# A third PSUM bank for projection tiles beside a recurrence, another order at the end of the attention, and more filling at one level

## The chip, the cores and the metric

The kernel runs on one NeuronCore of a Trainium2 chip. The metric is the device time of one execution in microseconds. TensorE (PE) multiplies matrices into PSUM, which is used here in banks of 128 x 512 float32; VectorE (DVE), ScalarE (ACT) and GpSimd (POOL) work on SBUF and PSUM, each through its own instructions in order; SyncE (SP) issues the DMA transfers.

## The reference, cut to what matters

One decoder layer over 16 meta tokens and 1024 tokens, D = 1024, all in float32. Four differential-attention heads and four heads of a gated linear recurrence (HGRN2) read one input projection; their outputs go side by side through an output projection, and a convolutional feed-forward part follows.

```python
a = rmsnorm(h, ln_mix_pre[l])
proj = a @ w_in[l]
dq, dk, dv, hq, hf, hi, hg = jnp.split(proj, SPLITS, axis=-1)
y_diff = diff_attention(dq, dk, dv, diff_lambda[l], diff_subln[l], rel_bias_table, lam_init)
y_hgrn = hgrn2(hq, hf, hi, hg, lb_all[l], hgrn_gnorm[l])
mix = jnp.concatenate([y_diff, y_hgrn], axis=-1) @ w_out[l]
h = h + rmsnorm(mix, ln_mix_post[l])
a = rmsnorm(h, ln_ffn_pre[l])
y = conv_ffn(a, w_ffn_up[l], ffn_conv_w[l], ffn_conv_b[l], w_ffn_down[l])
h = h + rmsnorm(y, ln_ffn_post[l])

# in diff_attention, for a block of 128 queries and a head, two maps m:
s = jnp.einsum('bhmqd,bhmkd->bhmqk', qblk, kh).astype(f32) * scale + bias[None, :, None]
s = jnp.where(dist >= 0, s, -jnp.inf)
p = jax.nn.softmax(s, axis=-1)
attn = p[:, :, 0] - lam * p[:, :, 1]
return jnp.einsum('bhqk,bhkd->bhqd', attn, vh)

# in hgrn2, for each position, with decay f = lb + (1 - lb) * sigmoid(f_logit):
S_new = jnp.exp(G_last)[..., None] * S + jnp.einsum(
    'bhsk,bhsv->bhkv', kh * jnp.exp(G_last[:, :, None] - G), vh)
```

## The kernel before, in words

A float32 product is made of three fp32r matmuls (high x high, low x high, high x low), so every weight tile is loaded, cast to its high half on ACT (`wh_...`), and its low half is a subtraction (`wl_...`, on POOL for the input projection, `wol...` on DVE for the output projection, where the high half is `woh...`).

The tokens lie in nine blocks: block 0 is the 16 meta tokens, the others 128 each. For the projections they make three groups of three blocks (`GROUPS`), of 272, 384 and 384 columns. A projection tile of a head (`dq`, `dk`, `dv` of the attention, `hf`, `hq`, `hi`, `hg` of the recurrence) is 24 matmuls per group into one PSUM bank, `pi_<name>_<group>` (`proj_group`, L231, and `proj_step`, L239). When the last of them is issued, the reading instructions follow: for dq, dk and dv ACT's casts to `q` and `k` and DVE's differences `q` and `kl`, or ACT's copy `vt`.

PSUM has eight banks: two are handed out in turn for the projection tiles (`ps_in`), two for small products (`ps_m`: `pl`, `pk`, `pu`, `pt`, `pa`, `E`), and four make two pairs for the scores and the recurrence's outputs (`ps_s`: `S`, `po`).

The order on TensorE is the order of the code. `interleave(dense, sides, fill, lead)` (L63) puts projection matmuls between the steps of a side: when a side yields a number c, matmuls for `fill` x c ns of nominal cost are issued, a matmul of 384 columns counting 161 and one of 272 counting 115; `FA, FH, FO` are 840, 800 and 800. The order on the other engines is chosen by the scheduler from the dependences, and each of them then runs its instructions one after another.

The main loop (L913 on) goes over the heads. The attention of head h is interleaved with the projection of the recurrence of head h; the recurrence of head h is interleaved with the projection of the attention of head h + 1, for heads 0 to 2. The recurrence of the last head is interleaved with the first part of the output projection (`py`, L988 to L992), whose token blocks are split in `mm<block>_<k>` (ACT's high half, DVE's low half) and read back through a DRAM buffer as `mp`.

In the recurrence (`hgrn_head`, L411) a tree of decay products is applied in seven levels. A level (`level`, L440 on) has 50 or fewer small matmuls `pl_<level>` of `kr` and `mix`, then multiplies `kr` by the decay (one instruction) and `mix` by it (one instruction for each of three groups, here called mix0, mix1 and mix2), and copies the results of the matmuls to `a` and `am`. The products of a level use the updates of the level before; each level ends with `yield 3`, so about 2400 ns of projection matmuls follow it. Behind level 7 three chains run side by side: transposes of `kr` (`pk`, L518), the state products (`pu`), the outputs (`po`) and their norms.

In the attention (`attn`) the last block of queries (block 8) has 1040 columns; its scores are in a pair of banks (`S`, 528 columns) and a small-product bank (`E`, 512 columns). Its maximum is the minimum of two negated maxima, one for `S` and one for `E` (`ast`, DVE, 128x1), and the two exponentials on ACT write the map `pb`. In the same stretch the transposes of block 7 (`pt_7`) are copied to `at_7` on DVE or ACT, and block 7's product `pa_7` follows. Behind that the two maps are combined on DVE (`pb`, 1040 columns) and block 8 is transposed.

Elsewhere in DVE's order stand the sums of the feed-forward weights (`wd`, one 128x512 addition at a time), and in POOL's order the splits `wl_...` of later tiles.

Of the kernel before, what the change touches and what calls it, by code (L numbers as in the profile page):

```python
# [13 lines left out]
ALU = mybir.AluOpType  # L14
# [12 lines left out]
NBLK = 9  # L27
# [7 lines left out]
FA, FH, FO = 840, 800, 800  # L35


def start(i):
    return 0 if i == 0 else META + P * (i - 1)


def rows(i):
    return META if i == 0 else P
# [17 lines left out]
def interleave(dense, sides, fill, lead=0):  # L61
    sides = list(sides)
    live = True  # L63

    def feed(budget):
        nonlocal live
        while live and budget > 0:
            c = next(dense, False)
            if c is False:
                live = False  # L70
            elif c is None:
                return
            else:
                budget -= c

    feed(lead)
    while sides:
        for s in list(sides):
            c = next(s, False)
            if c is False:  # L80
                sides.remove(s)
                continue
            feed(fill * (c or 1))
    feed(1e12)
# [3 lines left out]
def layer_kernel(ctx: ExitStack, tc: tile.TileContext, x, meta, table, lbl, gpre, gpost, win,  # L88
# [3 lines left out]
    V, A = Ordered(tc, nc.vector, state), Ordered(tc, nc.scalar, state)  # L92
# [53 lines left out]
    def ps_in(name):  # L146
        return pp.tile([P, 512], F32, tag="ip", name=name)
# [4 lines left out]
    def ps_s(name):  # L152
        return pp.tile([P, 2, 512], F32, tag="S", name=name)
# [70 lines left out]
    wd_sums = down_sums()  # L224
# [3 lines left out]
    def load_m(m, name, where=None, bufs=4):  # L228
        return [load_split(win[m][:, 512 * c: 512 * (c + 1)], f"{name}_{c}", where, bufs) for c in range(2)]

    def proj_group(g, parts, name, evac):  # L231
        b0, b1 = GROUPS[g]
        t0, t1 = start(b0), start(b1 - 1) + P
        n = t1 - t0
        pt = ps_in(f"pi_{name}_{g}")
        for k in range(KD):
            yield from proj_step(pt[:, :n], parts, k, t0, t1, lambda: evac(g, b0, b1, t0, t1, pt[:, :n]))

# [133 lines left out]
    def carried():  # L372
        tails = list(carry)
        carry.clear()
        return tails
# [37 lines left out]
    def hgrn_head(t, done=None):  # L413
        h, f, kr, vn = t["h"], t["f"], t["kr"], t["vn"]
# [88 lines left out]
        yield 3  # L503
        for lev in range(1, 8):
            level(lev)
            yield 3

        states = {0: None}

# [114 lines left out]
    def attn(h, tens):  # L624
        qs, ks, vn, rr = tens
        SY.dma_start(rr, rsc[h][127:127 + P * 383].rearrange("(p c) -> p c", c=383)[:, :256])
        pend = {}

        def scores(i):
            r = rows(i)  # L630
            q0 = start(i)
            W = q0 + r
            nm = f"{h}_{i}"
            pb = ap_.tile([P, 2, L], F32, tag="pb", name=f"pb{nm}", bufs=2)
            st = ap_.tile([P, 12], F32, tag="st", name=f"ast{nm}", bufs=3)
            pend[i] = pb
            nearw = min(256, W)
            j0 = P if i == 0 else 256 - nearw

            def qk_mm(dst, m, c0, n):  # L640
                T.matmul(dst, qs[m][:, q0:q0 + P], ks[m][:, c0:c0 + n], start=True, stop=False)
                T.matmul(dst, qs[m][:, q0:q0 + P], kl[m][:, c0:c0 + n], start=False, stop=True)

            nmx, sm, rc = st[:r, 0:2], st[:r, 2:4], st[:r, 4:5]
            if W <= 512:
                S = ps_s(f"S{nm}")
                for m in range(2):
                    qk_mm(S[:, m, :W], m, 0, W)
                near = S[:r, :, W - nearw:W]
                V.tensor_tensor(near, near, rr[:r, j0:j0 + nearw].rearrange("p (o c) -> p o c", o=1).to_broadcast([r, 2, nearw]), op=ALU.add)  # L650
                V.tensor_reduce(nmx, S[:r, :, :W], axis=AX.X, op=ALU.max, negate=True)
                for m in range(2):
                    A.activation(pb[:r, m, :W], S[:r, m, :W], AF.Exp, bias=nmx[:, m:m + 1], accum_out=sm[:, m:m + 1])
            else:
                for m in range(2):
                    S = ps_s(f"S{nm}_{m}")
                    hw = (W if W <= 912 else 528) // 2
                    for p_ in range(2):
                        qk_mm(S[:, p_, :hw], m, p_ * hw, hw)
                    mx = nmx[:, m:m + 1]  # L660
                    if W <= 912:
                        near = S[:r, 1, hw - 256:hw]
                        V.tensor_tensor(near, near, rr[:r], op=ALU.add)
                        V.tensor_reduce(mx, S[:r, :, :hw], axis=AX.XY, op=ALU.max, negate=True)
                        A.activation(pb[:r, m, :W].rearrange("p (a c) -> p a c", a=2), S[:r, :, :hw], AF.Exp, bias=mx, accum_out=sm[:, m:m + 1])
                    else:
                        E = ps_m(f"E{nm}_{m}")
                        qk_mm(E, m, 528, 512)
                        V.tensor_tensor(E[:r, 256:], E[:r, 256:], rr[:r], op=ALU.add)
                        ex = st[:r, 6 + 2 * m:8 + 2 * m]  # L670
                        V.tensor_reduce(ex[:, 0:1], S[:r, :, :hw], axis=AX.XY, op=ALU.max, negate=True)
                        V.tensor_reduce(ex[:, 1:2], E[:r], axis=AX.X, op=ALU.max, negate=True)
                        V.tensor_tensor(mx, ex[:, 0:1], ex[:, 1:2], op=ALU.min)
                        A.activation(pb[:r, m, :528].rearrange("p (a c) -> p a c", a=2), S[:r, :, :hw], AF.Exp, bias=mx, accum_out=ex[:, 0:1])
                        A.activation(pb[:r, m, 528:W], E[:r], AF.Exp, bias=mx, accum_out=ex[:, 1:2])
                        V.tensor_tensor(sm[:, m:m + 1], ex[:, 0:1], ex[:, 1:2], op=ALU.add)
                    if m == 0:
                        yield 0.7
            V.reciprocal(rc, sm[:, 1:2])
            V.scalar_tensor_tensor(rc, sm[:, 0:1], nlam[:r], rc, ALU.mult, ALU.mult)  # L680
            V.scalar_tensor_tensor(pb[:r, 0, :W], pb[:r, 1, :W], rc, pb[:r, 0, :W], ALU.mult, ALU.add)
            pend["sum", i] = sm[:, 0:1]
            yield 1.3 if W <= 512 else 0.7

        def values(i):
            r = rows(i)
            q0 = start(i)
            W = q0 + r
            nm = f"{h}_{i}"
            pb = pend.pop(i)  # L690
            pieces = [list(range(j, min(j + 4, i + 1))) for j in range(0, i + 1, 4)]
            ats = []
            for pi, blks in enumerate(pieces):
                pt = ps_m(f"pt{nm}_{pi}")
                at = ap_.tile([P, len(blks) if pi == 2 else 4, P], F32, tag=f"at{pi // 2}", name=f"at{nm}_{pi}", bufs=2 - pi // 2)
                for jj, j in enumerate(blks):
                    b = rows(j) if i == 0 else P
                    T.transpose(pt[:b, jj * r:(jj + 1) * r], pb[:r, 0, start(j):start(j) + b], ident[:r, :r])
                pv = pt.rearrange("p (j q) -> p j q", j=4)[:, :, :r] if r == P else None
                n0 = len(blks)  # L700
                if pi == 0:
                    A.copy(az[i % 2][:META, :r], pt[:META, :r])
                lo = 1 if pi == 0 else 0
                if n0 > lo:
                    (A.copy if pi % 2 else V.tensor_copy)(at[:, lo:n0], pv[:, lo:n0])
                ats.append(at)
                yield 0.8 if i < 4 else 0.6
            pend["ats"] = ats, pieces
# [44 lines left out]
                yield from values(i + 1)  # L753
        carry.append(pend.pop("tail"))

    def dense(tiles, preload=None, side=iter(())):
        parts = preload
        for idx, (m, name, evac) in enumerate(tiles):
            if parts is None:
                parts = load_m(m, name)  # L760
            nxt = load_m(tiles[idx + 1][0], tiles[idx + 1][1]) if idx + 1 < len(tiles) else None
            for g in range(3):
                next(side, None)
                for step, c in enumerate(proj_group(g, parts, name, evac)):
                    if step == 8:
                        flush()
                    yield c
            parts = nxt

    t_a, tiles = attn_in(0)  # L770
    parts = []
# [25 lines left out]
    pt = ps_m("pg")  # L797
# [12 lines left out]
    parts = [[None, None], [None, None]]  # L810
# [103 lines left out]
    for h in range(HEADS):  # L914
        t_h, tiles_h = hgrn_in(h)
        interleave(dense(tiles_h, None, wd_sums), [attn(h, t_a)] + carried(), FA, 1500)
        if h < HEADS - 1:
            t_a, tiles_a = attn_in(h + 1)
            interleave(dense(tiles_a, None, wd_sums), [hgrn_head(t_h)] + carried(), FH, 1500)

    assert next(wd_sums, wd_sums) is wd_sums
    line_up(hp, 24)
# [319 lines left out]
    for n, i in enumerate(order):  # L1242
# [38 lines left out]
        if i == 0:  # L1281
            low = qp.tile([P, 512], F32, tag="tmp", name="low", bufs=1)
# [477 lines left out]
```

## Time and profile before

| what | us |
|---|---|
| median of 3 runs | 1304.05 |
| the three runs | 1303.45, 1304.05, 1305.43 |
| the profiled execution's own time | 1303.76 |
| span of the profiled execution | 1302.0 |
| recurrences of heads 0 to 3 in it | 136 to 191, 263 to 317, 390 to 443, 517 to 577 |
| attention of heads 1 to 3 in it | 191 to 263, 317 to 390, 443 to 517 |
| feed-forward part | 660 to 1302 |

The profile shows one execution. Its own time lies 1.8 us over its span and 0.29 us under the median. A line of the timeline is a start in us, a duration in us, the engine, the line of the code, the operation, what it writes and reads, and the shape; in brackets stands the idle time of the engine just before it and what ended it. Most instructions of DVE and ACT go through one helper and so have its line, L54; they are told apart by their tiles. "xN" groups N such instructions. In the list of waits a row is the instruction, what it waited for, the total in us, the number of waits and the longest. A row of windows gives start and end, length, the busy time of PE, its weight loads, DVE, ACT and POOL, the granted clock, the DMA share and GB/s. A chain row is a start, a length and what the chain of work passed through.

### The profile page before, as it was taken

To read this page: it belongs to the slowest core of one execution; us is meant where nothing else is said; L and a number is where in the kernel's file an instruction comes from. 1 tells how busy PE (TensorE), PEld (TensorE's weight loads), DVE (VectorE), ACT (ScalarE), POOL (GpSimd) and SP (SyncE) were. 2 spreads that over 40 slices of the span, in tenths; PEclk is the share of its full clock that TensorE was granted. 3 is DMA by queue.
4 is the path that set the end of the run, shared out by engine and by line. 5 is a ranking of instruction groups with operands and counts; after the bars stand their busy time and mean duration, and the time that the engine had idled before them with its cause. 6 is when DMAs were issued, how large, how long until landed. Compare 5 with 4: busy or idle time off the path is not lost.

```text
span 1302.0 us, 26327 instructions
## 1 busy us (share of the span) xinstructions
PE 1270.9 (98%) x10236; PEld 1181.6 (91%) x10236; DVE 913.7 (70%) x1577; ACT 691.4 (53%) x1672; POOL 408.7 (31%) x322
## 2 busy tenths in 40 slices
PE   7999999999999999999999999999999999999997
PEld 6899999999998999777899999999999998888886
DVE  7575656575757565746888787787787787697587
ACT  7465356545653566446665454455455454454454
POOL 3211212021212120013155666766766740010020
PEclk9999999999999999999999999999999999999999
DMA  6221323122322211836711322222222236965363
GB/s 221 93 90 62 100 90 105 54 99 98 98 78 91 77 38 44 268 106 206 260 58 66 106 93 79 74 97 75 74 98 74 74 106 218 333 203 172 94 210 122
DMA packets 84371, 153.07 MB, mean 118 GB/s; under 512 B 9571, under 2 KB 19843, under 8 KB 84246
## 3 DMA queue, kind: packets, MB, share of 16 engines
q1 hardware_dynamic: 84246, 151.39, 35.2%
q8 instruction: 80, 1.31, 0.4%
q14 instruction: 45, 0.37, 0.1%
HBM read 112.69 MB, written 38.67 MB: 116 GB/s over the span
## 4 chain that ended last, share of the span: by engine, by line
PE 87%; DVE 6%; ACT 3%; DMA 2%; issue 1%; SPq 0%; DVEq 0%; ACTq 0%
PE pd L1571 5%; PE pd L1572 5%; PE pd L1570 5%; PE pb L1371 4%; PE pb L1372 4%; PE pb L1373 4%; PE pa L722 3%; PE pa L1372 3%; PE pa L1371 3%; PE pa L1373 3%; PE pc L1371 3%; PE pc L1373 3%; PE pc L1372 3%; PE pq L1350 2%; PE pq L1348 2%; PE pq L1349 2%
## 5 line engine op out<-in xcount | busy, mean ns | idle before, releaser
L1371 PE MATMUL pb<-t,uh 128*128 128x258 f32 (+1 forms) x456 | 127.4, 279 | 0.4 <-DVE u L54 0.4
L1372 PE MATMUL pb<-t,uh 128*128 128x258 f32 (+1 forms) x456 | 127.3, 279 | 0.0
L1373 PE MATMUL pb<-t,ul 128*128 128x258 f32 (+1 forms) x456 | 127.2, 279 | 0.0
L1571 PE MATMUL pd<-wl,gh 128*128 128x512 f32 (+1 forms) x314 | 120.8, 385 | 0.4 <-DVE wl L54 0.3
L1572 PE MATMUL pd<-wh,gl 128*128 128x512 f32 (+1 forms) x314 | 120.8, 385 | 0.0
L1570 PE MATMUL pd<-wh,gh 128*128 128x512 f32 (+1 forms) x314 | 120.7, 384 | 0.0
L54 DVE SCALAR_TENSOR_TENSOR c<-uu,cwt,c 128x512 f32<-128x512 f32 x88 | 94.7, 1077 | 22.3 <-ACT c L54 21.5
L1320 POOL TENSOR_TENSOR c<-c,c 128x512 f32<-128x512 f32 x44 | 64.4, 1463 | 127.2 <-ACT c L54 113.7
L54 DVE SCALAR_TENSOR_TENSOR c<-ug,cwt,c 128x512 f32<-128x512 f32 x88 | 84.0, 955 | 6.6 <-ACT c L54 5.9
L1371 PEld LDWEIGHTS pb<-t,uh 128*128 128x128 f32 x456 | 85.9, 188 | 0.8 <-DVE u L54 0.6
L1372 PEld LDWEIGHTS pb<-t,uh 128*128 128x128 f32 x456 | 85.9, 188 | 0.0
L1373 PEld LDWEIGHTS pb<-t,ul 128*128 128x128 f32 x456 | 85.8, 188 | 0.0
L1372 PE MATMUL pa<-t,uh 128*128 128x256 f32 (+1 forms) x304 | 85.3, 281 | 0.0
L1373 PE MATMUL pa<-t,ul 128*128 128x256 f32 (+1 forms) x304 | 85.2, 280 | 0.0
L1371 PE MATMUL pa<-t,uh 128*128 128x256 f32 (+1 forms) x304 | 85.2, 280 | 0.0
L1373 PE MATMUL pc<-t,ul 128*128 128x256 f32 x304 | 83.9, 276 | 0.0
L1371 PE MATMUL pc<-t,uh 128*128 128x256 f32 x304 | 83.9, 276 | 0.0
L1372 PE MATMUL pc<-t,uh 128*128 128x256 f32 x304 | 83.9, 276 | 0.0
L1571 PEld LDWEIGHTS pd<-wl,gh 128*128 128x128 f32 x314 | 59.0, 188 | 13.7 <-DVE wl L54 1.5
L1572 PEld LDWEIGHTS pd<-wh,gl 128*128 128x128 f32 x314 | 59.0, 188 | 12.0
L1570 PEld LDWEIGHTS pd<-wh,gh 128*128 128x128 f32 x314 | 59.0, 188 | 11.9
L54 ACT ACTIVATE c<-ug,cbt,cwt 128x512 f32<-128x512 f32 x44 | 35.9, 816 | 44.1 <-issue 26.2
(411 smaller groups left out, 4285.7 us busy)
## 6 DMA issues: line engine op xcount, KB each, us to landing
ra<-in_wup_dram SPq DMA_DIRECT2D x76, 256.0 KB, 2.7
wd<-in_wdown_dram SPq DMA_DIRECT2D x44, 256.0 KB, 3.3
tsc<-wd SPq DMA_DIRECT2D x44, 256.0 KB, 2.1
gsc<-c SPq DMA_DIRECT2D x44, 256.0 KB, 2.0
wi<-tsc SPq DMA_DIRECT2D x44, 256.0 KB, 3.0
gi<-gsc SPq DMA_DIRECT2D x33, 256.0 KB, 3.8
wi<-in_wdown_dram SPq DMA_DIRECT2D x33, 256.0 KB, 3.3
msc<-mm SPq DMA_DIRECT2D x21, 256.0 KB, 4.6
```

What stands on the lines that cost most here:

```text
L54: ins = call(*args, **kw)
L722: T.matmul(po[:, :P], w_, vn[:, j], start=(j == 0), stop=(j == i))
L1320: G.tensor_tensor(cg, cg, cu, op=ALU.mult)
L1348: T.matmul(pt, hi[:, s], th[:, k], start=(kh + k == 0), stop=False)
L1349: T.matmul(pt, hi[:, s], tl[:, k], start=False, stop=False)
L1350: T.matmul(pt, lo[:, s], th[:, k], start=False, stop=(kh == 1 and k == 3))
L1371: T.matmul(pt, hi[:, s], th[:, k], start=(first and k == 0), stop=False, skip_group_check=True)
L1372: T.matmul(pt, hi[:, s], tl[:, k], start=False, stop=False, skip_group_check=True)
L1373: T.matmul(pt, lo[:, s], th[:, k], start=False, stop=(k == 3), skip_group_check=True)
L1570: T.matmul(py, gh[:, s], wh, start=(k == 0 and pr not in (3, 7)), stop=False, skip_group_check=True)
L1571: T.matmul(py, gh[:, s], wl, start=False, stop=False, skip_group_check=True)
L1572: T.matmul(py, gl[:, s], wh, start=False, stop=(k == NH - 1), skip_group_check=True)
```

## The change

Three parts. First, in the recurrences of heads 0 to 2 the third group of each projection tile (g == 2) takes its bank from the score pairs instead of `ps_in`. Second, the copies of block 7 are issued after the minimum of block 8, and the combination of the two maps of block 8 is split in two instructions, of 400 and of 640 columns. Third, level 2 of every recurrence ends with `yield 4` instead of 3.

```diff
@@ proj_group
-    def proj_group(g, parts, name, evac):
+    def proj_group(g, parts, name, evac, wide=False):
         b0, b1 = GROUPS[g]
         t0, t1 = start(b0), start(b1 - 1) + P
         n = t1 - t0
-        pt = ps_in(f"pi_{name}_{g}")
+        pt = ps_s(f"pi_{name}_{g}")[:, 0] if wide and g == 2 else ps_in(f"pi_{name}_{g}")
@@ hgrn_head
         for lev in range(1, 8):
             level(lev)
-            yield 3
+            yield 4 if lev == 2 else 3
@@ scores
-                        V.tensor_tensor(mx, ex[:, 0:1], ex[:, 1:2], op=ALU.min)
+                        pend["low"] = V.tensor_tensor(mx, ex[:, 0:1], ex[:, 1:2], op=ALU.min)
...
-            V.scalar_tensor_tensor(pb[:r, 0, :W], pb[:r, 1, :W], rc, pb[:r, 0, :W], ALU.mult, ALU.add)
+            for c0, c1 in ((0, W),) if W <= 912 else ((0, start(4)), (start(4), W)):
+                V.scalar_tensor_tensor(pb[:r, 0, c0:c1], pb[:r, 1, c0:c1], rc, pb[:r, 0, c0:c1], ALU.mult, ALU.add)
@@ values
-                    (A.copy if pi % 2 else V.tensor_copy)(at[:, lo:n0], pv[:, lo:n0])
+                    with tc.issue_after(pend["low"].ins) if i == NBLK - 2 else nullcontext():
+                        (A.copy if pi % 2 else V.tensor_copy)(at[:, lo:n0], pv[:, lo:n0])
@@ dense
-    def dense(tiles, preload=None, side=iter(())):
+    def dense(tiles, preload=None, side=iter(()), wide=False):
...
-                for step, c in enumerate(proj_group(g, parts, name, evac)):
+                for step, c in enumerate(proj_group(g, parts, name, evac, wide)):
@@ main loop
-            interleave(dense(tiles_a, None, wd_sums), [hgrn_head(t_h)] + carried(), FH, 1500)
+            interleave(dense(tiles_a, None, wd_sums, True), [hgrn_head(t_h)] + carried(), FH, 1500)
```

At the end of head 0's attention DVE's order changes so (`ast_8` is the minimum where its row writes 128x1 from itself, `at_7` the copy of block 7, `pb_8` the combination):

```order
 L54 TENSOR_TENSOR E_8_1_1388<-E_8_1_1388,rr_139 128x256
 L54 TENSOR_REDUCE ast_8_1323<-E_8_1_1388 128x1
-L54 COPY at_7_0_1406<-pt_7_0_1405 128x384
 L54 TENSOR_TENSOR ast_8_1323<-ast_8_1323 128x1
+L54 COPY at_7_0_1407<-pt_7_0_1406 128x384
 L54 TENSOR_TENSOR wd_1_1187<-wd_1_1187,wd_1_1185 128x512
 L54 TENSOR_TENSOR ast_8_1323<-ast_8_1323 128x1
 L54 RECIPROCAL ast_8_1323<-ast_8_1323 128x1
 L54 SCALAR_TENSOR_TENSOR ast_8_1323<-ast_8_1323,nlam 128x1
-L54 SCALAR_TENSOR_TENSOR pb_8_1322<-pb_8_1322,ast_8_1323 128x1040
+L54 SCALAR_TENSOR_TENSOR pb_8_1322<-pb_8_1322,ast_8_1323 128x400
+L54 SCALAR_TENSOR_TENSOR pb_8_1322<-pb_8_1322,ast_8_1323 128x640
```

The minimum now stands ahead of the copy in heads 0, 1 and 2; in head 3 it stood there before.

TensorE in the recurrence of head 0, from the last projection matmuls ahead of level 3 on, before:

```order
L245 MATMUL pi_dq_2_1771<-alo_111,wh_dq_1_1596 128x384
L247 MATMUL pi_dq_2_1771<-ahi_108,wl_dq_1_1597 128x384
L243 MATMUL pi_dq_2_1771<-ahi_108,wh_dq_1_1596 128x384
L462 MATMUL pl_3_1836<-mix_99,kr_739 32x16 x8
L462 MATMUL pl_3_1836<-mix_100,kr_739 32x16 x12
L462 MATMUL pl_3_1836<-mix_101,kr_739 32x16 x12
L465 MATMUL pl_3_1836<-mix_99,kr_739 16x8
L245 MATMUL pi_dq_2_1771<-alo_111,wh_dq_1_1596 128x384
L247 MATMUL pi_dq_2_1771<-ahi_108,wl_dq_1_1597 128x384
L243 MATMUL pi_dq_2_1771<-ahi_108,wh_dq_1_1596 128x384
L245 MATMUL pi_dq_2_1771<-alo_111,wh_dq_1_1596 128x384
L247 MATMUL pi_dq_2_1771<-ahi_108,wl_dq_1_1597 128x384
```

and after the change:

```order
L245 MATMUL pi_dq_2_1772<-alo_111,wh_dq_1_1597 128x384
L247 MATMUL pi_dq_2_1772<-ahi_108,wl_dq_1_1598 128x384
L243 MATMUL pi_dq_2_1772<-ahi_108,wh_dq_1_1597 128x384
L245 MATMUL pi_dq_2_1772<-alo_111,wh_dq_1_1597 128x384
L247 MATMUL pi_dq_2_1772<-ahi_108,wl_dq_1_1598 128x384
L243 MATMUL pi_dq_2_1772<-ahi_108,wh_dq_1_1597 128x384
L245 MATMUL pi_dq_2_1772<-alo_111,wh_dq_1_1597 128x384
L247 MATMUL pi_dq_2_1772<-ahi_108,wl_dq_1_1598 128x384
L462 MATMUL pl_3_1846<-mix_99,kr_739 32x16 x8
L462 MATMUL pl_3_1846<-mix_100,kr_739 32x16 x12
L462 MATMUL pl_3_1846<-mix_101,kr_739 32x16 x12
```

Level 3's matmuls stand five projection matmuls later, behind the last of dq's third group; levels 4 to 7 and `pk` move with them. In the last head they stand three `py` matmuls later.

DVE at levels 6 and 7 of head 0, before:

```order
L54 TENSOR_TENSOR mix_101<-mix_101,tt_1637 128x6x32
L54 COPY am<-pl_6_2038 32x8x32 x2
L54 TENSOR_TENSOR kl_125<-pi_dk_1_1972,k_1_1584 64x384
L54 TENSOR_TENSOR kl_126<-pi_dk_1_1972,k_1_1585 64x384
L54 TENSOR_TENSOR wd_2_1619<-wd_2_1619,wd_2_1617 128x512
L54 TENSOR_TENSOR mix_99<-mix_99,tt_1637 128x2x64
L54 TENSOR_TENSOR kr_739<-kr_739,tt_1637 128x8x64
L54 TENSOR_TENSOR mix_100<-mix_100,tt_1637 128x3x64
L54 TENSOR_TENSOR mix_101<-mix_101,tt_1637 128x3x64
```

and after the change:

```order
L54 TENSOR_TENSOR mix_101<-mix_101,tt_1638 128x6x32
L54 TENSOR_TENSOR kl_125<-pi_dk_1_1973,k_1_1585 64x384
L54 TENSOR_TENSOR kl_126<-pi_dk_1_1973,k_1_1586 64x384
L54 TENSOR_TENSOR wd_2_1620<-wd_2_1620,wd_2_1618 128x512
L54 COPY am<-pl_6_2053 32x8x32 x2
L54 TENSOR_TENSOR mix_99<-mix_99,tt_1638 128x2x64
L54 TENSOR_TENSOR mix_100<-mix_100,tt_1638 128x3x64
L54 TENSOR_TENSOR kr_739<-kr_739,tt_1638 128x8x64
L54 TENSOR_TENSOR mix_101<-mix_101,tt_1638 128x3x64
```

The copies of `pl_6` moved behind both `kl` of dk's second group and the `wd` sum, and level 7's `kr` behind two updates of `mix` instead of one.

ACT in the last head's recurrence (`woh_6`, `woh_7` are the output projection's weights, `am` the copies of level 5, `mm_0` and `mm_4` the token block 8, `y` a copy of a finished `py`), before:

```order
L54 CAST mm_4_6877<-mix_101 128x384
L54 CAST woh_6_6929<-wor_6_6866 128x512
L54 COPY am<-a_6415 32x8x32 x4
L54 CAST mm_0_6908<-mix_101 128x512
L54 CAST woh_7_7010<-wor_7_6933 128x512
L54 COPY y_6305<-py_6_6806 128x512
```

and after the change:

```order
L54 CAST mm_4_6881<-mix_101 128x384
L54 CAST woh_6_6933<-wor_6_6870 128x512
L54 CAST woh_7_7014<-wor_7_6937 128x512
L54 COPY am<-a_6419 32x8x32 x4
L54 CAST mm_0_6912<-mix_101 128x512
L54 COPY y_6309<-py_6_6768 128x512
```

The cast `woh_7` moved ahead of the copies of `am` and of `mm_0`. On DVE in the same stretch the difference of `mm_4` for block 8, which stood ahead of level 7's `mix1` and `kr`, stands behind level 7, and that of block 7 moved from behind level 5's update of `kr` to ahead of it. On SP the load of that weight, `wor_7`, stands ahead of two transfers of `mm7` that it followed before.

## The prediction, made before the changed kernel ran

> **What bounds the kernel now.** I read the page's busy times first, then the chain of work that ended last, then the busy times by stage, then what TensorE waited for.
>
> ```profile
> PE 1270.9 (98%) x10236; PEld 1181.6 (91%) x10236; DVE 913.7 (70%) x1577; ACT 691.4 (53%) x1672; POOL 408.7 (31%) x322
> ...
> PE 87%; DVE 6%; ACT 3%; DMA 2%; issue 1%; SPq 0%; DVEq 0%; ACTq 0%
> ...
> 136.00:191.00 55.00, 53.41 (x752) 50.40 (x750) 35.73 (x80) 23.99 (x68) 11.54 (x14) 1.00 0.29 93
> ...
> 660.00:1302.00 642.00, 634.59 (x4594) 596.51 (x4592) 497.49 (x700) 324.05 (x640) 285.83 (x193) 1.00 0.37 123
> ```
>
> The kernel is bound by TensorE (98% busy, 87% of the chain, granted clock 1.00). The change adds and removes no matmul, so it can only take away or make moments in which TensorE stands still. Half of the span, the 642 us of the feed-forward part from 660 us on, isn't touched. What stays is the attention and recurrence half; one recurrence is the window of 55 us, in which TensorE is idle for 1.6 us. So single waits decide, a microsecond or less each:
>
> ```profile
> PE pl L462 <- DVE mix L54: 2.1, 3, 0.7
> PE pi_dv L243 <- DVE kl L54: 1.9, 3, 0.7
> PE pa L722 <- ACT pb L54: 1.9, 3, 0.8
> PE pk L518 <- DVE kr L54: 1.8, 1, 1.8
> ```
>
> Columns: total us, times, longest. These 10 waits with 7.7 us are what the change is near: pl (the level after 2), pi_dv (a projection bank), pa (the last attention block) and pk (last head). As lost TensorE time I count start to start, less the usual spacing, which is 0.1 to 0.3 more than each listed wait. That is also the ceiling of a gain, about 10 us.
>
> **A, the minimum ahead of the copy.** Heads 1 and 2 look alike; this is head 1.
>
> ```profile
> 240.94 0.16 DVE L54 TENSOR_TENSOR ast<-ast 128x1 f32<-128x1 f32 x1
> ...
> 245.68 0.69 DVE L54 TENSOR_REDUCE ast<-E 128x1 f32<-128x512 f32 x1
> 246.61 0.56 DVE L54 COPY at<-pt 128x384 f32<-128x384 f32 x1 [0.24 <-ACT az L54]
> 247.09 0.70 DVE L54 TENSOR_TENSOR ast<-ast 128x1 f32<-128x1 f32 x1
> ...
> 246.50 1.27 POOL L157 TENSOR_TENSOR wl_dq<-wr_dq,wh_dq 128x512 fp32r<-128x512 f32 x1 [3.47 <-ACT wh_dq L54]
> ...
> 248.51 0.68 ACT L54 ACTIVATE pb<-E,ast 128x512 f32<-128x512 f32 x1
> ...
> 249.34 0.49 PE L722 MATMUL pa<-avn,az 128*128 128x128 f32 x2 [0.83 <-ACT pb L54]
> ```
>
> The minimum stands behind the copy of block 7, which waits for ACT's az. It takes 0.70 instead of the 0.16 of the same operation at 240.94, and ends at 247.79, when POOL's wl_dq ends (246.50 + 1.27 = 247.77). The two exponentials follow at once, and pa, which takes the PSUM bank that the second one reads, starts 0.99 late from start to start. Moved up, the minimum can start at 246.40, 0.03 after the reduce ends as at 240.94, and ends at 246.56; ACT is then occupied with other copies until 246.95, the second exponential is through about 248.35 instead of 249.28, and pa is due at 248.35. So 0.9 in each of heads 1 and 2. In head 0 no POOL work stands in the way and pa loses 0.41, all of which goes; head 3 has the minimum in front already. The copy moves by under 0.1. **A = -2.2.** The margin is 0.10 us (246.40 against POOL's 246.50): were POOL first, the minimum would end at 247.77 as before, the copy behind it 1.2 later than now, and pa, behind the transposes that wait for that copy, 0.2 later than now (about 249.55): 0.2 lost in a head instead of 0.9 gained.
>
> The Trainium skill, "SBUF — State Buffer", section "Who interferes with whom", says that a DVE instruction with two SBUF inputs contends with a GpSimd instruction that reads SBUF. The trace agrees (0.70 against 0.16). The rule speaks against the change where POOL is first; that is the third rival, and by the other order A stays as it is.
>
> The split of the combination into 400 and 640 columns handles the same 1040. An extra operation costs between nothing and the 1.30 us of the whole at 249.96; I take 0.06. Its first reader, the transposes of block 8, comes 4 us later, which hides either.
>
> ```profile
> 255.31 0.60 PE L698 MATMUL pt<-ident,pb 128*128 128x128 f32 x4
> ```
>
> **B, the filling behind level 2** (head 0; PE, DVE and POOL).
>
> ```profile
> 151.43 0.34 PE L243 MATMUL pi_dq<-ahi,wh_dq 128*128 128x384 f32 x1
> 151.69 0.32 PE L462 MATMUL pl<-mix,kr 128*32 128x16 f32 x16
> 152.72 0.86 PE L462 MATMUL pl<-mix,kr 128*32 128x16 f32 x48 [0.71 <-DVE mix L54]
> ...
> 153.53 0.44 PE L245 MATMUL pi_dq<-alo,wh_dq 128*128 128x384 f32 x1
> ...
> 151.03 2.11 DVE L54 TENSOR_TENSOR mix<-mix,tt 128x136 f32<-128x136 f32 x3
> ...
> 151.16 1.29 POOL L157 TENSOR_TENSOR wl_dv<-wr_dv,wh_dv 128x512 fp32r<-128x512 f32 x1 [11.26 <-ACT wh_dv L54]
> ```
>
> Three mix updates take 2.11; the middle one alone takes 1.43 and ends with POOL's wl_dv (152.45). Level 3's matmuls stand at 152.72 in mid-row. With yield 4 five projection matmuls, 0.1735 each (the spacing below), go between: 0.87 of work that doesn't depend on mix. The stall is 0.89 + 0.27 (the second part for the third mix), 1.16, so 0.87 of it is filled. pl_3 then ends when it did, the later levels keep their times, and the projections are five matmuls further at each of them. **B = -0.87 x 3 = -2.6**, bounds 0 (the same stall one level on) and -3.5 (all of the 1.16).
>
> **C, the third bank.**
>
> ```profile
> 168.14 0.34 PE L243 MATMUL pi_dk<-ahi,wh_dk 128*128 128x384 f32 x1
> ...
> 169.53 0.34 PE L247 MATMUL pi_dk<-ahi,wl_dk 128*128 128x384 f32 x1
> ...
> 170.58 0.49 PE L518 MATMUL pk<-ident,kr 128*128 128x128 f32 x3
> ...
> 172.93 0.29 PE L247 MATMUL pi_dv<-ahi,wl_dv 128*128 128x272 f32 x1
> 173.96 0.41 PE L243 MATMUL pi_dv<-ahi,wh_dv 128*128 128x384 f32 x1 [0.74 <-DVE kl L54]
> ...
> 172.70 1.11 DVE L54 TENSOR_TENSOR kl<-pi_dk,k 64x384 fp32r<-64x384 f32 x2
> ```
>
> The nine pi_dk rows from 168.14 to 169.53 give 1.39 / 8 = 0.1735 a matmul. pi_dv group 1 takes the bank of dk group 2, whose last reader, the second kl, ends at 173.81; the matmul, due at 173.05, starts at 173.96, so 0.91 lost (0.58 and 0.91 in heads 1 and 2). After, dk_2 is in a score bank, and dv_1 takes the bank of dk_1, whose readers finish about 168. The score banks are free: no scores run in a recurrence, and po, which shares one, follows dq_2 by some 20 us; the next head's first scores stand behind the transposes of dv_2, so its bank's reader is done. **C = -2.4**, bounds -2.4 and 0 if something else holds dv_1.
>
> **D, level 7's kr comes later, pk doesn't.** DVE now has the copies of pl_6 behind both kl of dk_1 and the wd sum, and kr behind two mix updates instead of one.
>
> ```profile
> 165.12 0.84 DVE L54 COPY am<-pl 32x256 f32<-32x256 f32 x2
> 167.12 1.12 DVE L54 TENSOR_TENSOR kl<-pi_dk,k 64x384 fp32r<-64x384 f32 x2 [1.16 <-ACT k L54]
> 168.28 1.37 DVE L54 TENSOR_TENSOR wd<-wd,wd 128x512 f32<-128x512 f32 x1
> ...
> 169.77 0.68 DVE L54 TENSOR_TENSOR kr<-kr,tt 128x512 f32<-128x512 f32 x1
> ...
> 167.81 1.28 POOL L157 TENSOR_TENSOR wl_hf<-wr_hf,wh_hf 128x512 fp32r<-128x512 f32 x1 [11.25 <-ACT wh_hf L54]
> 170.47 1.39 POOL L157 TENSOR_TENSOR wl_hf<-wr_hf,wh_hf 128x512 fp32r<-128x512 f32 x1 [1.38 <-ACT wh_hf L54]
> ```
>
> Now kr ends at 170.45, in time for pk at 170.58. After: wd, the copies (0.84) and two mix updates go before. wd still ends with POOL's first wl_hf, which comes about 1 us earlier, at 168.7 as an estimate; the copies end at 169.4, mix0 at 169.6. POOL's second wl_hf follows dk_2's last matmul, five matmuls (0.87) earlier than its 170.47, so it starts near 169.6 and ends near 170.9: it holds mix1 or kr, as the first holds wd. kr then ends at 171.5 to 172.0 and pk, due still at 170.58, loses 0.9 to 1.4. In head 1 kr and POOL are 0.01 apart now, so 0 or 0.9. I take 1.2, 0.5 and 1.2. **D = +2.9**, bounds 0 (not held; there is no wait of pk here now that could go) and 4.2 (1.4 in each).
>
> **E, the last head.** There yield 4 moves everything three output-projection matmuls later, and with it the scheduler's order: ACT now takes woh1_7 ahead of the am copies and mm8_0, and DVE has mm8_4 behind kr.
>
> ```profile
> 549.40 1.64 ACT L54 COPY am<-a 32x256 f32<-32x256 f32 x4
> ...
> 555.13 0.62 ACT L54 CAST woh<-wor 128x512 fp32r<-128x512 f32 x1 [3.44 <-DMA wor<-in_wout_dram]
> ...
> 556.67 0.56 DVE L54 TENSOR_TENSOR mm<-mix,mm 128x384 fp32r<-128x384 f32 x1 [3.46 <-ACT mm L54]
> ...
> 555.94 0.40 PE L992 MATMUL py<-woh,mm 128*128 128x512 f32 x1
> 558.16 0.55 PE L518 MATMUL pk<-ident,kr 128*128 128x128 f32 x3 [1.82 <-DVE kr L54]
> ...
> 548.30 6.80 DMA wor<-in_wout_dram
> ```
>
> Before, kr sits behind DVE's mm8_4, which waits for ACT's mm8_4, which is behind woh1_7, which waits for a load issued at 548.30 and landed at 555.10. pk loses 1.98. After, mm8_4 is out of kr's way, but the am copies, mm8_0 and so kr's chain stand behind woh1_7: 0.62 + 1.64 + 0.62 on ACT, then mm8_0, wol, two mix and kr on DVE (0.69 + 0.68 + 0.28 + 0.35 + 0.69, less small overlaps), kr is there about 5.45 after the load lands. pk is due at 556.17 now (the last py row and its 0.23); three py more ahead of it would make 556.9, and I take 556.6 as the earlier side. The load waits for a buffer that wol1_4 frees, which DVE now does earlier, and on SP it stands ahead of the two mm7_0 transfers that it followed before: estimated landing 549.5 to 551, so no stall. A new one of about 0.45 comes at pl_6, behind mm7_4 on DVE. **E = -1.98 + 0.45 = -1.5**, bounds -2.0 and +2.4 (load landing at 555.1: kr at 560.55, a stall of 3.95).
>
> **Sum** -2.2 - 2.6 - 2.4 + 2.9 - 1.5 = -5.8. Against the profiled execution's own 1303.76 this gives 1297.96; it lies 0.29 under the median of 1304.05, so **1298.2**. The bounds together (D 0, E -2.0) give about 1295, and (D 4.2, E +2.4) about 1303.5.
>
> **The rivals.**
> - POOL doesn't hold level 7's kr (D 0 to 0.5, for the 0.01 us of head 1): 1295.5. Against it: both wl_hf follow the matmuls that move with the tile. 0.14.
> - The load of woh1_7 lands at 555.1 as before, since SP's earlier transfers hold it (E +2.4 instead of -1.5): 1302.1. For it: 6.80 us is a landing that has happened here. 0.17.
> - POOL's wl_dq starts ahead of the minimum in heads 1 and 2: A is then 0.2 lost in each of them against 0.4 gained in head 0, so its 2.2 go: 1300.4. A margin of 0.10 speaks for it nearly as much as against. 0.10.
> - The change moves the stalls but doesn't shorten the chain (each gap reappears one instruction later): 1303.5, 0.05.
> - Slower: the same ACT order, landing later than 557. There E is +4.3, which eats the rest of the sum; a load issued only when the transfer before it has landed (551.3) and taking 6.80 lands at 558.1 and gives 1305.2. Beyond 559.6 it is over 0.2% slower. 0.04.
>
> **How the numbers follow.** The forecast, with 1296.3 to 1299.8 as its own range, has 0.50. The measurement of this kernel can tell about 0.2%, 2.6 us: faster is under 1301.4, slower over 1306.7. The forecast, the first rival and the third (0.50 + 0.14 + 0.10) are faster, the second and the fourth (0.17 + 0.05) within it. Faster 0.74, same 0.22, slower 0.04. The range 1295.0 to 1302.4 reaches from the gains' bound to the second rival and leaves the last two out.
>
> **What would show it.** A: pa of block 8 loses under 0.2 in heads 1 and 2, and the minimum takes 0.16. B: no wait of pl on mix at level 3. C: no wait of pi_dv on kl. D: a new wait of pk on kr of about 1 us in heads 0 and 2. E: pk's wait in the last head gone, woh1_7 cast before 551. Wrong it is if the span beyond 660 us has another length, if the minimum takes 0.7 again, or if woh1_7's cast waits past 553.

## The result, and the profile after

| | median us | runs | range |
|---|---|---|---|
| before | 1303.45 | 7 | 1302.73 to 1305.43 |
| changed | 1299.37 | 7 | 1297.11 to 1300.37 |

The ratio is 0.9969, 95% interval 0.9958 to 0.9980: 4.1 us less, between 2.6 and 5.5. The forecast was 5.8 less, which is outside this interval. The profiled execution's span fell from 1302.0 to 1297.8.

First what TensorE waited for in the changed kernel (instruction, line, what it waited for, us in total, number, longest). Line numbers are those of the changed kernel, up to two higher than before; the rows of an experiment have those of its own kernel.

```profile
PE pk L518 <- DVE kr L54: 2.4, 2, 1.2
...
PE py L990 <- ACT woh L54: 1.5, 1, 1.5
PE py L990 <- DMA mp<-msc: 1.1, 2, 0.7
...
PE pl L456 <- DVE kr L54: 0.7, 1, 0.7
...
PE ss L580 <- DVE on L54: 0.2, 1, 0.2
```

Three of the four rows of before are gone: pl on mix, pi_dv on kl, pa on pb. The row of pk has stayed but is another one: two waits of 1.2 in place of one of 1.8. The rows py, pl on kr and ss are the last head and the output projection.

The end of the attention in head 1 (timeline; start, duration, then what is written and read):

```profile
245.71 0.16 DVE L54 TENSOR_TENSOR ast<-ast 128x1 f32<-128x1 f32 x1
245.91 0.56 DVE L54 COPY at<-pt 128x384 f32<-128x384 f32 x1
...
245.80 1.27 POOL L157 TENSOR_TENSOR wl_dq<-wr_dq,wh_dq 128x512 fp32r<-128x512 f32 x1 [3.46 <-ACT wh_dq L54]
...
247.51 0.29 PE L245 MATMUL pi_hg<-alo,wh_hg 128*128 128x272 f32 x1
247.65 0.49 PE L724 MATMUL pa<-avn,az 128*128 128x128 f32 x2
```

The minimum takes 0.16 and starts 0.09 ahead of POOL's subtraction; pa follows the projection matmul at its usual spacing.

Levels 3 and 7 and the second group of dv in head 0 (PE, DVE, POOL):

```profile
151.83 0.34 PE L247 MATMUL pi_dq<-ahi,wl_dq 128*128 128x384 f32 x1
152.10 1.05 PE L462 MATMUL pl<-mix,kr 128*32 128x16 f32 x64
...
173.06 0.29 PE L247 MATMUL pi_dv<-ahi,wl_dv 128*128 128x272 f32 x1
173.19 0.34 PE L243 MATMUL pi_dv<-ahi,wh_dv 128*128 128x384 f32 x1
...
168.37 0.85 DVE L54 COPY am<-pl 32x256 f32<-32x256 f32 x2
169.25 1.63 DVE L54 TENSOR_TENSOR mix<-mix,tt 128x128 f32<-128x128 f32 x2
170.81 0.68 DVE L54 TENSOR_TENSOR kr<-kr,tt 128x512 f32<-128x512 f32 x1
...
169.19 1.28 POOL L157 TENSOR_TENSOR wl_hf<-wr_hf,wh_hf 128x512 fp32r<-128x512 f32 x1 [1.40 <-ACT wh_hf L54]
...
170.06 0.28 PE L245 MATMUL pi_dv<-alo,wh_dv 128*128 128x272 f32 x1
171.54 0.55 PE L518 MATMUL pk<-ident,kr 128*128 128x128 f32 x3 [1.19 <-DVE kr L54]
```

Level 3's matmuls follow their projections (0.28 start to start is lost inside the row, for the third mix), and dv's last group starts in its turn. The new wait is the third group of rows: the two mix updates, started 0.06 behind POOL, end 0.41 behind it, kr ends at 171.49 and pk starts 1.35 late. It is the same in head 2; in head 1 pk doesn't wait. There kr and POOL start closer together:

```profile
295.04 0.69 DVE L54 TENSOR_TENSOR kr<-kr,tt 128x512 f32<-128x512 f32 x1
...
295.02 1.85 POOL L157 TENSOR_TENSOR wl_hf<-wr_hf,wh_hf 128x512 fp32r<-128x512 f32 x1 [1.92 <-ACT wh_hf L54]
```

kr starts 0.02 behind POOL and isn't held (0.69); POOL's subtraction is, with 1.85 in place of 1.28.

The last head (PE, ACT):

```profile
543.27 0.62 ACT L54 CAST woh<-wor 128x512 fp32r<-128x512 f32 x1 [4.52 <-DMA wor<-in_wout_dram]
546.38 0.62 ACT L54 CAST woh<-wor 128x512 fp32r<-128x512 f32 x1 [1.06 <-DMA wor<-in_wout_dram]
...
546.04 0.92 PE L456 MATMUL pl<-mix,kr 128*32 128x32 f32 x32 [0.66 <-DVE kr L54]
...
553.79 0.49 PE L518 MATMUL pk<-ident,kr 128*128 128x128 f32 x3
```

woh1_7 is cast at 546.38, 8.75 earlier than before, and pk doesn't wait. pl of level 6 does, and loses 0.83: its kr stands on DVE behind mm7_4, that behind ACT's, and that behind woh1_5 (543.27), whose load took 5.24 us. Both rows are as forecast in kind.

### The profile page after: what moved, and what is told of

It is laid out like the page before. It is cut to its first block, busy times and chain, and to the rows that moved or that the text cites. A ratio compares the mean times of both kernels' runs of the same rounds, so it can differ in the third digit from the quotient of the medians.

```text
span 1297.8 us, 26325 instructions
## 1 busy us (share of the span) xinstructions
PE 1270.1 (98%) x10236; PEld 1181.0 (91%) x10236; DVE 916.4 (71%) x1581; ACT 689.5 (53%) x1672; POOL 408.5 (31%) x322
## 3 DMA queue, kind: packets, MB, share of 16 engines
q8 instruction: 80, 1.31, 0.4%
## 4 chain that ended last, share of the span: by engine, by line
PE 54%; DVE 2%; DMA 1%; ACT 1%; issue 0%; DVEq 0%; ACTq 0%
PE pd L1573 5%; PE pd L1574 5%; PE pd L1572 5%; PE pb L1373 4%; PE pb L1374 4%; PE pb L1375 4%; PE pa L1374 3%; PE pa L1375 3%; PE pa L1373 3%; PE pc L1373 3%; PE pc L1375 3%; PE pc L1374 3%; PE pq L1352 2%; PE pq L1350 2%; PE pq L1351 2%; PE py L990 1%
```

## The experiments

Theory: each part is worth what its own waits lost, the parts add up, and the filling in heads 0 to 2 brings the wait at pk with it through POOL's hold. The rivals stand with each run. Each kernel was timed beside the kernel before; differences are from the ratio, with its 95% interval.

**The parts alone.** The minimum and the split alone (the diff of scores and values, nothing else):

> Only the second part of the change (the minimum of block 8 ahead of the copies of block 7, the combination split in two); banks and filling as before. Theory that the parts add up: pa's losses of 0.41, 0.99 and 0.99 in heads 0 to 2 go, the rest stays, 2.4 us less than before (1.9 to 2.9). Rival, that the wait only moves to the transposes of block 8 or into the recurrence that follows: 0 to 0.8 less, with a new wait of that size between block 7's product and the first level of the recurrence.

Measured: ratio 0.9973 [0.9964, 0.9983], 3.5 less [2.2, 4.7]; medians 1299.51 against 1302.75. The waits of pa on pb are gone, those of pl and pi_dv stand as before, and no new one has come in the recurrences. In the last head and behind it the waits differ, though its code is that of before: pk doesn't wait, and py waits 1.7 for its `mp` instead of 0.8 (see the last experiment). The theory's 2.4 lies in the interval, the rival's 0.8 doesn't.

The bank alone:

```diff
+        pt = ps_s(f"pi_{name}_{g}")[:, 0] if wide and g == 2 else ps_in(f"pi_{name}_{g}")
```

> Only the first part (third group of the projection tiles in a score bank in the recurrences of heads 0 to 2). Theory that the bank's wait is worth what it lost: pi_dv's 0.91, 0.58 and 0.91 go, level 7's kr stays in time for pk since DVE's order stays, 2.4 us less than before. The waits at level 3 (1.16 lost in each of three heads) stay. Rival, that the projections run ahead into the same kl or another reader: 0 to 0.8 less.

Measured: 0.9980 [0.9971, 0.9989], 2.6 less [1.4, 3.8]. pi_dv's waits on kl are gone, those of pl on mix (2.1, three) stay. The theory holds.

The filling alone, in heads 0 to 2:

```diff
-            yield 3
+            yield 4 if lev == 2 and done is None else 3
```

> Only the third part, and only in heads 0 to 2 (yield 4 behind level 2; two banks in turn, old end of the attention, last head as before). Theory that level 7's kr is the filling's own price: 0.88 gained at level 3 in each of three heads, 1.35 lost at pk in heads 0 and 2, pi_dv still short of its bank though a little less than before: between 1.0 less and 0.8 more than before. Rival, that the new wait of pk came from the bank or from the minimum: 2.6 less, no wait of pk on kr.

Measured: 1.0007 [0.9998, 1.0015], 0.9 more, from 0.3 less to 2.0 more. The waits of TensorE in this kernel:

```profile
PE pk L518 <- DVE kr L54: 2.4, 2, 1.2
...
PE pi_dv L243 <- DVE kl L54: 1.8, 3, 1.2
```

No row of pl on mix is left, and the same two waits of pk have come, without the bank and without the minimum. So the wait at pk belongs to the filling, which alone gains nothing that shows. In head 1, where pk doesn't wait, pi_dv's wait has grown from 0.42 to 1.20; in heads 0 and 2 it has fallen from 0.74 to 0.28 and 0.29.

The filling alone, in the last head (the same line with `done is not None`):

> Only the third part, and only in the last head's recurrence. Theory that the reordering there is worth what its own waits say: pk's 1.98 goes, pl of level 6 gets 0.83 and a ss wait 0.38, nothing at the first py wait (520 us) or the mp wait (611 us), 0.8 us less than before (0.3 to 1.3). Rival, that those two waits belong to the reordering too: 0.1 more than before (0 to 0.3 more), with both waits longer.

Measured: 1.0003 [0.9995, 1.0012], 0.4 more, from 0.7 less to 1.6 more. The rival's 0.1 more lies in the interval, the theory's 0.8 less just outside it, though its range reaches in, and the forecast's 1.5 less is out. In this kernel's trace pk doesn't wait, nor does pl of level 6, and the first py wait (on woh) is 1.4, against 1.1 before. The theory that takes these waits as steady falls here; the one put in its place, that they come and go with the landing of loads, is tried below.

**Without the filling, and without the last head's.** The changed kernel with `yield 3` everywhere:

> The changed kernel without its third part (yield 3 behind level 2 everywhere): minimum and bank alone. Theory that the filling in heads 0 to 2 costs more at pk than it gains and is worth nothing in the last head: 2.5 + 2.6 = 5.1 us less than before (4.3 to 5.9), so about 0.8 less than the changed kernel, with the waits at level 3 back and none of pk in heads 0 and 2. Rival, that the filling pays: 2.4 to 3.3 less than before.

Measured: 0.9963 [0.9950, 0.9976], 4.8 less [3.1, 6.5]. That is the theory's number, but the interval reaches 3.1 and so takes in a part of the rival: by times alone the third part is worth nothing that shows. In the traces TensorE is 5.4 us ahead of before at the end of head 3's attention without the filling and 4.3 with all parts, so 1.1 for leaving it out. Of this 0.35 is there at the first level of head 0, ahead of any filling; the 0.75 that is left is near the theory's 0.8.

The changed kernel with `yield 3` in the last head alone:

> The changed kernel with yield 3 in the last head. Theory that the last head's part is worth nothing, since the wait of pk there comes and goes with the landing of one weight load from execution to execution: as the changed kernel, 4.1 less than before (3.4 to 4.8). Rival, that the forecast's 1.5 is there: 2.6 less than before.

Measured: 0.9965 [0.9952, 0.9978], 4.6 less [2.9, 6.3]: as the changed kernel. The rival's 2.6 is just outside.

**The cause of the wait at pk.** Level 7 in another order on DVE, in heads 0 to 2; first kr only ahead of the mix updates:

```diff
-            V.tensor_tensor(k4[:, :, 0, :], k4[:, :, 0, :], pr[:, :, 1:2].to_broadcast([P, n // (2 * hb), hb]), op=ALU.mult)
-            for b0, b1 in GROUPS:
...
+            up = V.tensor_tensor(k4[:, :, 0, :], k4[:, :, 0, :], pr[:, :, 1:2].to_broadcast([P, n // (2 * hb), hb]), op=ALU.mult)
+            first = lev == 7 and done is None
+            with tc.issue_after(up.ins) if first else nullcontext():
+                for b0, b1 in GROUPS:
```

> The changed kernel with DVE's level 7 in another order in heads 0 to 2: kr ahead of the mix updates, still behind the copies of level 6. Theory that POOL's second wl_hf holds whatever DVE operation of two SBUF inputs starts behind it: kr (free to start at about 169.25, POOL at 169.19) is held until POOL ends at 170.47, so kr lasts about 1.8 and pk still loses about 0.9 in heads 0 and 2; 0.9 less than the changed kernel, 5.0 less than before (4.3 to 5.9). Rival, that only the order counts: kr takes 0.68 and is done at 169.95, pk loses nothing, 2.7 less than the changed kernel.

Measured: 0.9955 [0.9943, 0.9967], 5.9 less [4.3, 7.4], which takes in the 5.0 of the theory and the 6.8 of the rival; the trace tells them apart. Timeline of head 0:

```profile
169.41 1.75 DVE L54 TENSOR_TENSOR kr<-kr,tt 128x512 f32<-128x512 f32 x1
...
169.33 1.28 POOL L157 TENSOR_TENSOR wl_hf<-wr_hf,wh_hf 128x512 fp32r<-128x512 f32 x1 [1.38 <-ACT wh_hf L54]
...
171.21 0.55 PE L520 MATMUL pk<-ident,kr 128*128 128x128 f32 x3 [0.73 <-DVE kr L54]
```

kr starts 0.08 behind POOL and takes 1.75 in place of 0.68; pk loses 0.88, as the theory said, and not the rival's nothing. The Trainium skill, "SBUF — State Buffer", section "Who interferes with whom", has the rule (a DVE instruction with two SBUF inputs contends with a GpSimd instruction that reads SBUF), and the trace agrees; the price is of this trace, about 0.55 beyond POOL's end.

Then kr directly behind the wd sum, and the copies of level 6 (kept back in the list `keep`) behind kr:

```diff
+            for dst, src in keep:
+                with tc.issue_after(up.ins):
+                    up = V.tensor_copy(dst, src)
+            behind = bool(keep)
+            keep.clear()
+            with tc.issue_after(up.ins) if behind else nullcontext():
+                for b0, b1 in GROUPS:
```

> The changed kernel with kr of level 7 directly behind the wd sum, the copies of level 6 behind kr, and then the mix updates, in heads 0 to 2. Theory of POOL's hold: kr starts at 168.4, ahead of POOL's 169.19, ends at 169.05, pk finds it and the bank of level 6 free; 2.7 less than the changed kernel, 6.8 less than before (5.8 to 7.8). Rival, that pk then waits for the copies of level 6, whose bank it takes, or that pi_dv or pu waits instead: 0 to 1 less than the changed kernel.

Measured: 0.9955 [0.9943, 0.9967], 5.9 less [4.3, 7.4], with the theory's 6.8 in the interval, and most of the rival's 4.1 to 5.1 too; again the trace tells them apart. Timeline of head 0:

```profile
168.35 0.68 DVE L54 TENSOR_TENSOR kr<-kr,tt 128x512 f32<-128x512 f32 x1
169.04 0.85 DVE L54 COPY am<-pl 32x256 f32<-32x256 f32 x2
...
169.26 1.29 POOL L157 TENSOR_TENSOR wl_hf<-wr_hf,wh_hf 128x512 fp32r<-128x512 f32 x1 [1.38 <-ACT wh_hf L54]
...
170.25 0.49 PE L530 MATMUL pk<-ident,kr 128*128 128x128 f32 x3
```

kr takes 0.68 again, done before POOL starts, and pk no longer waits, in any head. The copies, whose source is PSUM, run beside POOL from 169.26 to 169.89 and take their usual 0.85. The work and the POOL operation are the same; only the order changed. So the cause is shown: POOL's subtraction holding the DVE operations that stand between the copies and pk.

Three kernels beside each other to settle the size, the changed one among them:

> The changed kernel once more, beside the two below on one chip: 4.1 us less than before (2.6 to 5.5).

> The changed kernel with level 7's kr directly behind the wd sum, once more. Theory of POOL's hold: 2.7 less than the changed kernel beside it (1.7 to 3.7). Rival, that the time saved in the recurrences is lost again at the weight loads of the output projection: under 1 less than the changed kernel.

> The same with yield 3 in the last head. Theory that the last head's filling is worth nothing on the mean: as the kernel before it, within 1 us. Rival, that it saves pk's wait there: 1.5 more than the kernel before it.

| kernel | median us | range | ratio to before [95%] |
|---|---|---|---|
| changed kernel | 1298.52 | 1297.38 to 1300.77 | 0.9968 [0.9955, 0.9980] |
| with kr early | 1296.31 | 1294.17 to 1296.91 | 0.9944 [0.9930, 0.9957] |
| with kr early, last head with yield 3 | 1295.77 | 1294.32 to 1296.36 | 0.9940 [0.9928, 0.9953] |

kr early is worth 2.2 by the medians (2.7 was expected; the ranges don't overlap), and the last head's filling again nothing. The third kernel has the lowest median, 7.1 us under before (1302.83 in these runs), but its range overlaps with that of the second.

**The last head, over all executions.** The code of the last head was as before in six of the experiments' kernels and in the kernel before, as changed in the others. In e_bank and e_min, the bank alone and the minimum alone, the last head's code is that of before (ACT's woh1_7 and PE's pk of each; a row of DMA is the time from issue to landing):

```profile
547.03 5.88 DMA wor<-in_wout_dram
...
552.94 0.62 ACT L54 CAST woh<-wor 128x512 fp32r<-128x512 f32 x1 [2.64 <-DMA wor<-in_wout_dram]
...
555.97 0.55 PE L518 MATMUL pk<-ident,kr 128*128 128x128 f32 x3 [1.82 <-DVE kr L54]
```

```profile
548.88 0.62 ACT L54 CAST woh<-wor 128x512 fp32r<-128x512 f32 x1 [0.53 <-DMA wor<-in_wout_dram]
...
553.00 0.49 PE L518 MATMUL pk<-ident,kr 128*128 128x128 f32 x3
```

The first of these fences is the bank alone: pk waits 1.82, just as before. The second is the minimum alone: the load had landed and pk doesn't wait. Of the seven profiled executions with the old code two show the wait, those in which this load took longest, 6.80 and 5.88 us from issue to landing; in the other five it took 3.67 to 4.53. From the last head's first pl to the first matmul of the feed-forward part (pq; 530.36 to 642.51 in the trace of before) the seven take 110.09 to 112.37 us, mean 111.10, and the six with the new order 110.46 to 111.84, mean 111.07. By their spread the difference of these means is known to about 1 us, which leaves out a gain of 1.5.

## Why the prediction was right, and where it was off

The time lies in the forecast's range and the sign was right, but the 5.8 became 4.1. The forecast stood on a median of 1304.05 before, which over seven runs is 1303.45; so its time is off by 1.2 and its difference by 1.7, and that the time still fell into the range is owed in part to the width of the range. By steps, start to start in the profiled execution:

| step | forecast | in the trace |
|---|---|---|
| A, the minimum ahead of the copy | -2.2 | -2.4 (0.41, 0.99, 0.99 gone) |
| B, level 3's stall in three heads | -2.6 | -2.6 (0.88 each) |
| C, the bank | -2.4 | -2.4 (0.91, 0.58, 0.91 gone) |
| D, the new wait at pk | +2.9 | +2.7 (1.35, 0, 1.35) |
| E, the last head | -1.5 | nothing on the mean |

- A to D came out by mechanism and by size, and experiments bear each out: A and C alone give their amounts, B alone brings D, and D is undone by an order that gets kr out of POOL's way. The margin of 0.10 at the minimum was 0.09. The split of the combination cost DVE 0.13 (1.43 for the two, 1.30 for the one before) and not the 0.06 that the forecast took, for which no row stands; nothing waited for it. Of D two readings were off without harm to the sum: the wd sum ends 0.56 behind POOL's first subtraction (169.65 against 169.09) and not with it, and it was mix0 already that POOL held, one operation earlier than the forecast's mix1 or kr. Head 1, which the forecast left open at 0.01 and entered with 0.5, fell on the good side. What was not foreseen: TensorE gains 1.8 in the three recurrences by landmarks (the shift of its matmuls grows from 0.46 at the first level of head 0 to 4.28 after head 2, less the 2.0 of the two attention ends), where B, C and D sum to 2.3. The remaining 0.5 is spread over changes of tile that are too small to assign. It goes with the filling: from the same mark on, the shift agrees with the waits to 0.2 in the traces of the bank alone, the minimum alone and both, and 0.7 is missing with the filling alone.
- E is the step that failed, and it is the term "E = -1.98 + 0.45 = -1.5". Its order of instructions came out: pk's wait went, pl of level 6 got one, of 0.83 in place of 0.45. But 1.98 wasn't a cost of the kernel; it was what one execution lost to a load that took 6.80 us to land. The same code of the last head, in seven kernels profiled once each, shows no such wait in five. The new wait of pl hangs on a load as well: among the six executions with the new order it stands in the two in which the load of woh1_5 took 5.24 and 5.37 us, and in none of the four in which it took 4.08 to 4.49. So the 1.5 couldn't be gained, and the kernels that differ only in the last head have the same time. The forecast took a wait behind a DMA from the one profiled execution as if it were as steady as one behind an engine. Why the load takes longer in some executions stays open; and as no kernel with the old order was profiled twice, that its landing differs between executions of one program, and not only between kernels whose last head is alike, isn't shown.
- Of the rivals, the one in which POOL doesn't hold level 7's kr was wrong, that in which it is first at the minimum didn't happen, and none of the others came about. woh1_7 was cast at 546.38, which on the clock of before (4.3 us later) is 550.7, within the 549.5 to 551 of the forecast.

## What to carry to other kernels

Most waits behind another engine repeated here to a tenth of a microsecond from trace to trace and could be counted; a wait that ends with the landing of a load can't, until more than one execution shows it. More filling ahead of a wait moves everything that follows on the other engines too: look up which later wait the same matmuls move under, since the filling here paid for itself only after kr was taken out of POOL's way (by the traces: at the end of head 3's attention TensorE is then 6.9 us ahead of before, with no filling 5.4; the times, 5.9 less and 4.8 less, don't separate the two). And where a short DVE operation and a POOL operation start within a tenth of a microsecond of each other, the order decided about a microsecond here.

## What the runs showed of the hardware

The landing time of one and the same weight load (256 KB, from issue to landing) went from 3.67 to 6.80 us over seven executions of code that is alike there, while the waits behind engines ahead of it repeated: level 3's loss was 0.88 or 0.89 in every head of every kernel that had it, and pa's 0.98 or 0.99 in heads 1 and 2. An exception is pk in heads 0 and 2 where POOL holds it back: it lost 1.31 to 1.35 seven times and 1.06 once (e_no_last, head 2), where both mix updates were ahead of POOL and kr itself was held, for 1.78.

A DVE operation on 128x512 with two SBUF inputs that started 0.08 to 0.47 us behind POOL's subtraction ended 0.54 or 0.55 behind the end of it, whenever it had started: the wd sum ahead of level 7 in heads 0 to 2 of every trace, and kr in heads 0 and 2 of e_kr_first and in head 2 of e_no_last. In head 1 of the changed kernel it is the other way: kr takes its 0.69 and POOL's subtraction 1.85 in place of 1.28, though the profile has POOL's start 0.02 ahead. So starts as close as this don't tell which of the two is held.
